# Seven-product pairs of an encoder layer: running sums kept in a PSUM bank instead of added on VectorE

## The chip, the cores and the metric

The kernel runs on one core of one Trainium2 chip. The time is device microseconds of that core, for one launch that computes the whole layer for both batches of requests. Engines are called as the profile calls them: PE is TensorE's matmul, PEld its loading of weights, DVE is VectorE, ACT is ScalarE, POOL is GpSimd, and SP is SyncE, whose queue issues nearly all transfers.

## The reference

One encoder layer is computed for two batches with the same weights: `x_prompt` with 512 tokens and `x_sample` with 1024 tokens, both 1024 channels wide. All of it is float32.

```python
def encoder_layer(x, norm_g, w_in, ..., w_o_a, w_o_b, w_out, t5_table):
    h = rmsnorm(x, norm_g)
    proj = h @ w_in
    qa, ka, va, za, qb, kb, vb, zb, ga, gb = jnp.split(proj, ...)
    ...
    oa = neighbourhood_attention(qa, ka, va, rpb_a) * jax.nn.silu(za)
    oa = oa @ w_o_a
    ...
    ob = window_gqa_attention(qb, kb, vb, t5_table, sink_b) * jax.nn.silu(zb)
    ob = ob @ w_o_b
    merged = jax.nn.sigmoid(ga) * oa + jax.nn.sigmoid(gb) * ob
    return x + merged @ w_out
```

What matters here are the dense products: `z` (8 chunks of 128 output channels), the gates `g` (16 chunks) and the output `w_out` (8 chunks), each with 1024 input channels.

## The kernel before, in words

**Precision.** Every float32 operand is split into a high part in the type that PE takes and the low rest (`split`, line 1161 onward: ACT makes the high part at L1167, DVE or POOL the rest at L1172). A block of 128 input channels then costs three matmuls: high weight by high data, high weight by low data, low weight by high data (`product`, L1284 to L1286). One such step of three is one operation of the planner.

**Stages.** Attention of the short batch, its dense phase, attention of the long batch, its dense phase. A dense phase computes the z chunks, then the gates, then the merge (`w_o_a`, `w_o_b`, times the gates), then the output. Two output chunks are taken together as a pair. With `CLASSIC_P = (4, 8, 4)` all pairs of the short batch are classic: one PSUM bank for each chunk and half of the tokens, eight steps each. With `CLASSIC_S = (1, 0, 2)` the long batch takes 3 z pairs, 6 gate pairs and 2 output pairs with seven products instead of eight (`pair_strassen`): a 2 by 2 block product in which weights and data are first summed, and the products are combined afterwards. These eleven are called Z1 to Z3, G0 to G5, O2 and O3.

**A pair of seven products.** The raw weights of two chunks (two tiles each) are loaded; four sums S are made of them, and the seven operands are split into five of the six `whi`/`wlo` buffers, so the next pair's first tile has one to itself. The data side is either the normalized input `hh`/`hl` itself or one of four sums T of its blocks (T0 to T3). For the z and gate pairs these were stored to DRAM in an earlier stage by `norm_pair` and are loaded by `stored_sums`, through the four buffers of tile U; for the output pairs `sums` makes them on DVE and POOL. A product has 512 columns and four steps, 12 matmuls. In the order of the weights the products are P0 to P6. Before the change each one has a PSUM bank of its own:

- P0 is copied by ACT into p1 (a U tile, L1354); result (0,0) is p1 + P1.
- u2 = p1 + P2, u3 = u2 + P3, u4 = u2 + P4, each a DVE add into a U tile.
- result (1,1) is u3 + P4, result (1,0) is u3 - P5, result (0,1) is u4 + P6.

In the output pairs (`seed`) the residual x is loaded into a C tile, the U value is added, then the bank. In the last pair P6 is cut into two halves of 256 columns, in two banks, so that the first half can be stored while the second is computed.

**What follows a result** (`post`). A z result goes through Silu on ACT, is multiplied with the attention output loaded into `ot` (two buffers; two loads, which are added first, for the chunks of Z2 and Z3) and is stored. A gate goes through Sigmoid and is stored. An output is stored.

**Order of the work.** `Flow` takes all operations with their dependences, priorities and estimated durations, and plans them ahead: whenever an engine is free in its plan, it takes the ready operation with the lowest priority number, and among equals the one created first. The resulting order of each engine is then fixed. A pair's operations all carry the pair's priority, its weights half a unit less, so a later pair's operation fills in where the earlier pair has nothing ready. Tiles with the tags in `IN_TURN` (weights, T, S, raw, U, C, ot) are given out strictly in the order in which they were created in the program. The plan keeps two engines off one PSUM value at the same time (`locked`): an engine waits until the other's operation on it has ended.

**Banks.** PSUM has eight banks, handed out by `ROTA = "ppxxxxxd"`: two called p, five called x, one d. `bank(next(tags))` takes the next name, so the name of a bank in a profile row tells products apart.

## Time and profile before

| what | us |
|---|---|
| median of three timed runs | 1146.3 |
| lowest and highest of them | 1145.42 and 1147.29 |
| span of the profiled execution, first to last instruction | 1144.7 |
| PE busy in it | 1133.8 |
| PEld, DVE, ACT, POOL busy | 985.8, 854.4, 644.9, 308.3 |
| pairs Z1 to G5 of the long batch | 800.2 to 971.6 |
| first product of O2 | 1103.23 |

The profile is of one execution; for it the page gives the span and no other time. A row of the timeline has the start in us, the length in us, the engine, the source line, the operation, output tile <- input tiles with shapes, and in brackets how long the engine stood idle before it and what ended that idle time. A row of the waits has the waiting engine and line, the one it waited for, the total in us, how often, and the longest. A row of the stretches has start:end and length, then for PE, PEld, DVE, ACT and POOL the busy time and the number of instructions, then PE's granted clock (1.00 is full), the busy share of the DMA engines, and GB/s. A row of a tile has the line, engine, operation and number of instructions, then shortest, median and longest in ns, then the first and last start. A row of the chain of waits has start, length and what it was. SPq is the queue of SP, where a transfer is issued; lines 1354 and 1161 are the lines of helpers and copies: L1161 is every two-operand add, subtract or multiply of the dense phases. Matmuls overlap: one with 512 columns is shown as 0.39 us long, but the next starts 0.23 us after it.

### The profile page before, as it was taken

How to read it: one execution, taken by the hardware profiler on the slowest of the kernel's cores; microseconds unless marked ns; L12 is line 12 of the kernel's file. 1: busy time of each engine (PE TensorE's matmuls, PEld its weight loads, DVE VectorE, ACT ScalarE, POOL GpSimd, SP SyncE). 2: the span in 40 equal slices, each digit the busy share in tenths (PEclk: the TensorE clock that was granted, in tenths of full speed). 3: DMA queues.
4: the chain of work that ended last, by engine and by line, in shares of the span. 5: the costliest groups of instructions: out<-in, count | busy, mean ns of one | idle time of the engine just before them, and what ended most of it. 6: DMA issues, size and time to landing. Idle time of an engine off the chain costs nothing.

```text
span 1144.7 us, 18482 instructions
## 1 busy us (share of the span) xinstructions
PE 1133.8 (99%) x6139; PEld 985.8 (86%) x6139; DVE 854.4 (75%) x1975; ACT 644.9 (56%) x1467; POOL 308.3 (27%) x413
## 2 busy tenths in 40 slices
PE   8999999999999999999999999999999999999998
PEld 6999988888888899999999888888888888788887
DVE  5888798497765468887778888865878755497984
ACT  5777987544433346665678988865534434343320
POOL 3653433000010054343333445330222210132110
PEclk9999999999999999999999999999999999999999
DMA  7854543488786422121221213226657335573072
GB/s 253 273 158 141 181 113 102 115 264 266 232 277 199 165 72 67 25 70 32 71 61 50 56 37 93 56 66 214 218 148 211 129 111 159 200 238 121 29 223 90
DMA packets 124705, 159.86 MB, mean 140 GB/s; under 512 B 28297, under 2 KB 66961, under 8 KB 124610
## 3 DMA queue, kind: packets, MB, share of 16 engines
q1 hardware_dynamic: 124610, 158.69, 45.4%
q8 instruction: 48, 0.79, 0.3%
q14 instruction: 47, 0.39, 0.1%
HBM read 121.93 MB, written 41.44 MB: 143 GB/s over the span
## 4 chain that ended last, share of the span: by engine, by line
PE 94%; DVE 2%; DMA 2%; ACT 1%; POOL 1%; issue 0%; SPq 0%; ACTq 0%; POOLq 0%
PE p L761 25%; PE x L1285 9%; PE x L1286 9%; PE x L1284 9%; PE x L1063 5%; PE x L1026 5%; PE x L934 4%; PE p L1284 4%; PE p L1285 4%; PE d L1284 4%; PE p L1286 4%; PE d L1286 4%; PE d L1285 4%; PE x L861 2%; DMA ot<-u_d 1%; DMA w<-in_w_att_dram 1%
## 5 line engine op out<-in xcount | busy, mean ns | idle before, releaser
L761 PE MATMUL p<-whi,hh 128*128 128x384 f32 x384 | 133.4, 348 | 0.0
L761 PE MATMUL p<-wlo,hh 128*128 128x384 f32 x384 | 133.1, 347 | 0.0
L761 PE MATMUL p<-whi,hl 128*128 128x384 f32 x384 | 132.4, 345 | 0.0
L978 ACT ACTIVATE sb<-sb,mx 128x384 f32<-128x384 f32 (+1 forms) x192 | 107.5, 563 | 22.4 <-DVE mx L969 22.2
L1167 ACT ACTIVATE whi<-raw 128x512 fp32r<-128x512 f32 (+1 forms) x140 | 81.1, 590 | 52.6 <-PE x L1285 26.2
L761 PE MATMUL p<-whi,hb 128*128 128x384 f32 x384 | 107.5, 347 | 0.0
L1172 POOL TENSOR_TENSOR wlo<-raw,whi 128x512 fp32r<-128x512 f32 (+1 forms) x29 | 40.9, 1413 | 242.4 <-ACT whi L1167 130.4
L1284 PE MATMUL x<-hh,whi 128*128 128x512 f32 x264 | 102.7, 389 | 0.0
L1285 PE MATMUL x<-hl,whi 128*128 128x512 f32 x264 | 102.7, 389 | 0.0
L1286 PE MATMUL x<-hh,wlo 128*128 128x512 f32 x264 | 102.7, 389 | 0.0
L1037 DVE TENSOR_TENSOR pp<-x,pp 128x512 fp32r<-128x512 f32 (+1 forms) x136 | 82.6, 638 | 18.9 <-ACT pp L1032 17.8
L1172 DVE TENSOR_TENSOR wlo<-raw,whi 128x512 fp32r<-128x512 f32 (+1 forms) x111 | 70.1, 645 | 30.5 <-ACT whi L1167 30.2
L1285 PE MATMUL x<-T,whi 128*128 128x512 f32 x224 | 87.5, 390 | 0.3 <-DVE T L1172 0.2
L1286 PE MATMUL x<-T,wlo 128*128 128x512 f32 x224 | 87.2, 389 | 0.0
L1284 PE MATMUL x<-T,whi 128*128 128x512 f32 x224 | 87.1, 389 | 0.0
L1032 ACT ACTIVATE pp<-x 128x512 fp32r<-128x512 f32 (+1 forms) x136 | 70.9, 560 | 22.8 <-PE x L1026 21.8
L799 POOL TENSOR_TENSOR rs_r<-rs_v,mhalf 128x4 f32<-128x4 f32 (+1 forms) x72 | 81.7, 1134 | 5.7
L1063 PE MATMUL x<-pp,v 128*128 128x256 f32 (+1 forms) x368 | 77.8, 324 | 0.8 <-DVE pp L1037 0.8
L792 POOL TENSOR_SCALAR rs_v<-ss 128x4 f32<-128x4 f32 (+1 forms) x72 | 26.2, 364 | 187.3 <-DVE ss L785 184.6
L761 PEld LDWEIGHTS p<-whi,hl 128*128 128x128 f32 x384 | 73.0, 190 | 1.3 <-issue 1.0
L761 PEld LDWEIGHTS p<-wlo,hh 128*128 128x128 f32 x384 | 73.0, 190 | 1.0 <-issue 0.5
L761 PEld LDWEIGHTS p<-whi,hh 128*128 128x128 f32 x384 | 73.0, 190 | 0.9 <-issue 0.5
(351 smaller groups left out, 2985.5 us busy)
## 6 DMA issues: line engine op xcount, KB each, us to landing
raw<-in_w_g_dram SPq DMA_DIRECT2D x76, 256.0 KB
w<-in_w_att_dram SPq DMA_DIRECT2D x46, 384.0 KB
ot<-o_d SPq DMA_DIRECT2D x36, 256.0 KB
g_d<-C SPq DMA_DIRECT2D x34, 256.0 KB
raw<-in_w_z_dram SPq DMA_DIRECT2D x32, 256.0 KB
raw<-in_w_out_dram SPq DMA_DIRECT2D x32, 256.0 KB
C<-g_d SPq DMA_DIRECT2D x24, 256.0 KB
out_dram<-C SPq DMA_DIRECT2D x23, 256.0 KB
```

The lines of the kernel that those rows point to most:

```text
L761: pe.matmul(ps.t[:, :GW], part[u](k), mv.t[:, c], start=k == 0 and m == 0, stop=k == KC - 1 and m == 2,)
L799: lambda e: nc.gpsimd.tensor_tensor(r.t[:, :nn], rv.t[:, :nn], mhalf[:, :nn], op=ALU.pow),
L978: act.activation(sb.t[:, :width], sb.t[:, :width], AF.Exp, bias=mx.t[:, i : i + 1], scale=-1.0, accum_out=sm.t[:, i : i + 1],)
L1026: pe.transpose(pt.t[:, u * P : (u + 1) * P], sbs[i].t[:, c * P : (c + 1) * P], ident)
L1032: lambda e, pt=pt, pp=pp, nn=nn: act.activation(pp.t[:, 0, :nn], pt.t[:, :nn], AF.Copy),
L1037: lambda e, pt=pt, pp=pp, nn=nn: dve.tensor_tensor(pp.t[:, 1, :nn], pt.t[:, :nn], pp.t[:, 0, :nn].bitcast(F32), op=ALU.subtract),
L1063: pe.matmul(out(), v.t[:, vs], mv(), start=first, stop=last)
L1167: (("act", ACT_(n)),), lambda e: act.activation(hi(), src(), AF.Copy), prio,
L1172: lambda e: engines[e].tensor_tensor(lo(), src(), hi().bitcast(F32), op=ALU.subtract), prio,
L1284: pe.matmul(out, hi.t[:, cs], mh(), start=first and k == 0, stop=False)
L1285: pe.matmul(out, hi.t[:, cs], ml(), start=False, stop=False)
L1286: pe.matmul(out, lo.t[:, cs], mh(), start=False, stop=last and k == len(ws) - 1)
```

## The change

In a pair of seven products P2, P3 and P5 are accumulated into the bank that holds P0. Between them ACT copies the bank to p1, u2 and u3, which are now plain copies. P4 moves ahead of P3 and has a second bank, from which result (1,1) reads; then P6 is accumulated into that bank, and result (0,1) is u2 plus it. Result (1,0) is read straight from the first bank. u4 and four DVE adds a pair are gone; the pair takes three banks instead of seven. In the last pair both halves of P6 go into the second bank. So that P5 can be added, T3 changes its sign, in `norm_pair` and in `sums`. A parameter `kept` comes with its branches, but no call sets it.

```diff
@@ norm_pair
-            (3, (1, 1), (1, 0), (1, 0)),
+            (3, (1, 0), (1, 1), (1, 0)),
@@ sums
-                step(3, lambda v=t[1]: v.t[:, :sn], (1, 0), 0, ALU.subtract, True, t[1])
-                step(3, lambda v=t[3]: v.t[:, :sn], (1, 0), 1, ALU.subtract, False)
+                after = done[k + 4, 0] if done else []
+                tt(
+                    lambda v=t[3]: v.t[:, :sn], h[1, 0, 0], lambda v=t[1]: v.t[:, :sn], ALU.subtract, sn, prio,
+                    new=[t[3]], use=[t[1]], after=after, hold=[hh],
+                )
+                step(3, lambda v=t[3]: v.t[:, :sn], (1, 0), 1, ALU.add, False)
@@ product
-        def product(ps, ws, movs, prio, first, last, after=(), n=nh):
+        def product(ps, ws, movs, prio, first, last, after=(), n=nh, at=0, again=False):
...
-                    out = ps.t[:, :n]
+                    out = ps.t[:, at : at + n]
...
+                    more = {"skip_group_check": True} if again else {}
@@ pair_strassen
-            p1, u2, u3, u4 = (tile_("U", 4, sn) for _ in range(4))
+            p1, u2, u3 = (tile_("U", 4, sn) for _ in range(3))
...
+            def mul(i, mov, ps=None, after=()):
+                fresh = ps is None
+                ps = ps or bank(next(tags))
+                h_reads.append(product(ps, w[i], mov, prio, fresh, True, [opened, *after], sn, again=not fresh))
                 return ps
...
+            def partial(out, ps):
...
+                return f.op(
+                    (("act", ACT_(sn, False)),), lambda e: act.activation(out.t[:, :sn], ps.t[:, :sn], AF.Copy), prio,
+                    new=[out], use=[ps],
+                )
...
-            result(0, 0, p1, mul(1, mov_h(1, 0)))
-            add(u2, p1, mul(2, mov_t(1)))
-            add(u3, u2, mul(3, mov_t(2)))
-            b = mul(4, mov_t(0))
-            add(u4, u2, b)
-            result(1, 1, u3, b)
-            result(1, 0, u3, mul(5, mov_t(3)), ALU.subtract)
+                x = mul(0, mov_h(0, 0))
+                o = partial(p1, x)
+                result(0, 0, p1, mul(1, mov_h(1, 0)))
+                x = mul(2, mov_t(1), x, [o])
+            o = partial(u2, x)
+            z = mul(4, mov_t(0))
+            x = mul(3, mov_t(2), x, [o])
+            o = partial(u3, x)
+            read = result(1, 1, u3, z)
+            x = mul(5, mov_t(3), x, [o])
...
+                post(1, 0, sn, x, True, prio)
             if not last:
-                result(0, 1, u4, mul(6, mov_h(1, 1)))
+                result(0, 1, u2, mul(6, mov_h(1, 1), z, [read]))
                 return
...
-                product(ps, w[6], movs, prio, True, True, n=nh // 2)
+                o = product(z, w[6], movs, prio, False, True, [read], nh // 2, s.start, True)
                 tt(
-                    lambda s=s: c.t[:, s], lambda s=s: c.t[:, s], lambda ps=ps: ps.t[:, : nh // 2], ALU.add, nh // 2,
-                    prio, psum=True, use=[ps], hold=[c], after=c.writers[:],
+                    lambda s=s: c.t[:, s], lambda s=s: c.t[:, s], lambda s=s: z.t[:, s], ALU.add, nh // 2,
+                    prio, psum=True, hold=[c, z], after=[*c.writers[:], o],
                 )
```

## The prediction

> **What bounds the kernel now.** I read the page first: span, busy shares, the chain of work that ended last. The span of this one execution is 1144.7 us; the three timed runs have a median of 1146.3, so I sum against the span and add 1.6 at the end.

> ```profile
> span 1144.7 us, 18482 instructions
> ...
> PE 1133.8 (99%) x6139; PEld 985.8 (86%) x6139; DVE 854.4 (75%) x1975; ACT 644.9 (56%) x1467; POOL 308.3 (27%) x413
> ...
> PE 94%; DVE 2%; DMA 2%; ACT 1%; POOL 1%; issue 0%; SPq 0%; ACTq 0%; POOLq 0%
> ```

> PE is busy 99% and carries 94% of the chain: TensorE is the bound, and 10.9 us of the span are not its work. Second, the waits of PE, over the whole span and from 785 us on (the dense stage of the 1024-token batch, the only one with pairs of seven products, since the short batch's setting is all classic).

> ```profile
> PE x L1629 <- DMA rb<-in_norm_row_dram: 4.4, 1, 4.4
> ...
> PE x L1285 <- DVE T L1172: 0.2, 1, 0.2
> ```

> The large wait is at the start of the program; in the stage that changes there is one, of 0.2 us. Third, the busy time by stretches, each one pair long, and the stretch where the gates give way to the merge.

> ```profile
> 819.30:838.30 19.00, 19.00 (x85) 15.74 (x84) 12.35 (x20) 5.71 (x12) 4.49 (x3) 1.00 0.64 191
> ...
> 970.00:990.00 20.00, 19.66 (x85) 15.44 (x84) 9.78 (x15) 6.86 (x12) 1.62 (x1) 1.00 0.80 282
> ```

> PE (third column) fills its pair wholly at granted clock 1.00. Only 970 to 990 is short: 85 matmuls where 20 us hold 20/0.227 = 88, and gaps that I add up in the timeline to 1.1 us. So DVE and ACT time in these pairs is free now, and no removed DVE add can shorten the end by itself. The most this change could win is that 1.1 us.

> **The change part by part.** I call the products of a pair P0 to P6 by their weight operand, and the pairs Z1 to Z3, G0 to G5, O2, O3: eleven.

> Removed: u2, u3 and u4 on DVE, and one add for the result c10.

> ```profile
> L1161 DVE TENSOR_TENSOR U<-U,x x21: 674/683/689, 815.4 to 1136.1; 128x512 f32<-128x512 f32 x21
> ...
> L1161 DVE TENSOR_TENSOR U<-U,p x7: 680/687/689, 817.2 to 966.7; 128x512 f32<-128x512 f32 x7
> L1161 DVE TENSOR_TENSOR U<-U,d x5: 672/683/689, 816.6 to 1118.3; 128x512 f32<-128x512 f32 x5
> ```

> 21+7+5 = 33 adds, three a pair; with c10's, 44 at 0.68 = 30 us of DVE. ACT gains two copies a pair, 22 at 0.60 = 13 us. Both lie beside PE's work (in Z2 DVE is busy 12.35 and ACT 5.71 of 19.00), so both count as nothing as busy time; what they cost or give through the order of the queues is counted below. Behind a copy in ACT's queue stand silus and the next weight splits, which wait for nothing new unless PE is late. The matmuls stay the same in number and form, so PE's work stays. The T3 sign swaps operands in a subtract of the same shape, and `sums` keeps two instructions for it: nothing either way. No DMA is added; x loads of c10 in O pairs stay.

> What it adds is **waits of PE on the evacuation**. Before, each product has its own bank. Now P2 waits for the copy of P0's sum, P3 for that of P2's, P5 for that of P3's, and P6 for the add of c11 that reads P4's bank. Behind a waiting matmul stands all of PE. The price of one such wait without cover:

> ```profile
> 1124.77 0.39 PE L1286 MATMUL x<-hh,wlo 128*128 128x512 f32 x1
> ...
> 1125.25 0.60 ACT L1354 ACTIVATE U<-x 128x512 f32<-128x512 f32 x1 [5.04 <-PE x L1286]
> ...
> 975.01 0.69 DVE L1172 TENSOR_TENSOR T<-ot,T 128x512 fp32r<-128x512 f32 x1 [0.67 <-ACT T L1167]
> ...
> 975.76 0.50 PE L1285 MATMUL x<-T,whi 128*128 128x512 f32 x1 [0.22 <-DVE T L1172]
> ```

> The last matmul of P0 starts at 1124.77; an idle ACT copies from 1125.25 to 1125.85; a result reaches a waiting PE 0.06 later (975.70 to 975.76). PE could go on at 1125.91 instead of 0.23 after the last start: **0.91 us**. Covers: P1 stands between P0 and P2, P4 between P2 and P3, each 2.72 us (two products from 800.23 to 805.67, quoted below), so the copy may be 1.8 late. Between P3 and P5 nothing of the pair is left; the planner takes whatever is ready, so two steps of the next pair's P0 (0.68 each, 1.36) if its weights are there. P6 has P5 (2.72) against one add of 0.69.

> *The end, O3.* No pair follows, so P3 to P5 is bare: 0.91.

> ```profile
> 1140.03 0.28 PE L1284 MATMUL p<-hh,whi 128*128 128x256 f32 x1
> ...
> 1140.28 0.42 DVE L1161 TENSOR_TENSOR C<-C,p 128x256 f32<-128x256 f32 x1 [0.80 <-PE p L1286]
> ...
> 1141.35 0.28 PE L1286 MATMUL p<-hh,wlo 128*128 128x256 f32 x1
> ...
> 1141.66 0.42 DVE L1161 TENSOR_TENSOR C<-C,p 128x256 f32<-128x256 f32 x1 [0.96 <-PE p L1286]
> ```

> Now the add of the first half (1140.28) runs while PE writes the second half into another bank. With both halves in one bank the planner's lock keeps DVE off until PE is done with the bank; the first add then moves behind 1141.63 and pushes the last by its 0.42. Bounds 0 and 0.42; I take 0.4, as the lock is in the code. End: **1.3**. [...]

> *The start, Z1.*

> ```profile
> 800.23 0.39 PE L1284 MATMUL x<-hh,whi 128*128 128x512 f32 x1
> ...
> 801.96 0.93 ACT L1167 ACTIVATE whi<-raw 128x512 fp32r<-128x512 f32 x2
> ...
> 805.67 0.39 PE L1284 MATMUL x<-T,whi 128*128 128x512 f32 x1
> ...
> 811.61 1.32 DVE L1172 TENSOR_TENSOR T<-U,T 128x512 fp32r<-128x512 f32 x2 [0.30 <-ACT T L1167]
> ...
> 812.34 0.60 ACT L1354 ACTIVATE U<-x 128x512 f32<-128x512 f32 x1
> ```

> P0 ended at 802.95, yet its copy came at 812.34: tile U has four buffers in turn, and the sixteen loads of the T sums stand first; the copy gets a buffer when DVE frees one (811.61+0.69 = 812.30). Today P2 goes on at 805.67 regardless. Then it must wait until 813.0, 7.3 us. Ready in between: P4 (2.72), and P0 and P1 of Z2, whose weights are made at 801.96 (5.44): 8.16. So no idle there, but this spends the later covers: 0.91 each before P3 and P5, less the 0.8 left over: **1.0**. Bounds 0, and 3 if P1 of Z2 isn't ready.

> *The lag, Z2 to G1.* Silu results wait for two loads each through two ot buffers.

> ```profile
> DVE ot L1161 <- DMA ot<-o_d: 11.7, 5, 3.9
> ...
> 840.80 0.39 PE L1286 MATMUL x<-hh,wlo 128*128 128x512 f32 x1
> ...
> 845.14 0.63 ACT L1387 ACTIVATE C<-C 128x512 f32<-128x512 f32 x1 [2.04 <-DVE C L1161]
> 845.68 0.58 ACT L1354 ACTIVATE U<-x 128x512 f32<-128x512 f32 x1
> ...
> 859.84 0.39 PE L1286 MATMUL p<-hh,wlo 128*128 128x512 f32 x1
> ...
> 865.69 0.58 ACT L1354 ACTIVATE U<-p 128x512 f32<-128x512 f32 x1
> ...
> 917.45 0.60 ACT L1354 ACTIVATE U<-x 128x512 f32<-128x512 f32 x1 [0.59 <-PE x L1286]
> ```

> DVE stands 11.7 us on the ot loads between 812 and 892; ACT stands on DVE; P0's copy stands behind that in ACT's queue. A copy 0.48 after the last matmul would be at 841.28 in Z3 and 860.32 in G0; it came 4.4 and 5.4 late. Free banks swallow that now; PE would stand for it less 0.4 to 1.8 of cover, at most 5.0 in all (a stall once taken makes the next smaller). Against it DVE loses 4 x 0.68 = 2.7 a pair. If both of Z2 and Z3 count, nothing is left; I count one, since DMA waits do not shrink with DVE work: 5.0-2.7 = **2.3**, bounds 0 and 5. In G3 the copy waits for PE itself (917.45): G2 to G5 cost 0.

> *The merge.* Its T tiles reuse those of the sums: T1 free after P2, T2 after P3, which now comes after P4.

> ```profile
> 963.40 0.63 ACT L1167 ACTIVATE T<-ot 128x512 fp32r<-128x512 f32 x1 [1.57 <-PE d L1285]
> ...
> 964.95 0.32 SPq L1537 DMA_DIRECT2D ot<-u_d  x1
> ...
> 967.11 4.66 DMA ot<-u_d
> ...
> 973.18 4.96 DMA ot<-u_d
> ```

> 963.40 becomes 2.72 later. Two ot buffers are taken in turn, so the load at 967.11 follows the one released there (964.95 becomes 967.7) by an SP issue: near 968.0. It feeds the next, at 973.18, and that the matmul after it: **0.9**. Bounds -1.1 (today's gaps gone) and 2.7.

> *O2.* The copy stands behind a split that waits for a late load.

> ```profile
> 1108.21 0.42 ACT L1167 ACTIVATE whi<-raw 128x256 fp32r<-128x256 f32 x1 [3.88 <-DMA raw<-in_w_out_dram]
> ...
> 1108.53 0.58 ACT L1354 ACTIVATE U<-x 128x512 f32<-128x512 f32 x1
> ...
> 1108.67 0.39 PE L1284 MATMUL x<-T,whi 128*128 128x512 f32 x1
> ```

> Done at 1109.11, plus 0.06, against 1108.67: **0.5**, bounds 0 and 0.5.

> Sum: 1.3+1.0+2.3+0.9+0.5 = 6.0. Span 1150.7, time 1152.3. All lower ends give about -0.2 (1146.1), all upper ends 12.5 (1158.8).

> **The rivals.** *Covered:* only the end shows, 1147.6 (+0.1%), not slower. Place: Z2 to G1. It decides where the relief of DVE brings the copies to within 1.8 us of PE. For it: 2.7 us a pair in a stretch where DVE has no slack, and a planner that fills gaps; against it: the waits on ot loads, and a planner whose order is fixed ahead and met loads later than planned. *Bare:* every bank re-entered shows its 0.91: 33 x 0.91 + 0.4 = 30.4, 1176.7. [...] Against bare: P1 and P4 lie between. *Faster:* needs more than 2.3 us, while the pairs hold 1.1. That DVE's adds do not go, or that the sums are not kept in one bank, nothing in the code suggests.

> **How the numbers follow.** About 0.2% (2.3 us) is what a measurement of this kernel tells from no change. Forecast, 1148.6 to 1159: 0.66; worse than 1159 short of bare 0.03; bare 0.03; covered, within 0.2%: 0.25; faster 0.03. Slower 0.72. The range 1147 to 1159 leaves out the two upper cases, the faster one and the lowest part of covered, some 2 in 10.

> **What would show it.** Right: PE waits on ACT U at P2, P3 or P5, about 0.9 in the last pair and above that in Z1 to G1; DVE some 30 us less busy; ACT 13 more; a first-half add behind the last matmul. P3 after P4 in the PE order. Wrong: no PE wait before 1120 us, or one at P6 on DVE that is larger than those on ACT, or fewer matmuls.

## The result, and the profile after

The changed kernel takes 1158.1 us (median of six runs, 1156.9 to 1159.5) against 1146.8 for the kernel before in the same session (six runs, 1145.4 to 1155.2): a ratio of 1.0095, with an interval of 1.0077 to 1.0113, so slower by 8.8 to 13.0 us. The forecast was 1152.3, in a range of 1147 to 1159. The direction was right and the time lies in the range; the size was too small, 6.0 us forecast and 10.4 to 11.3 found. The profiled execution has a span of 1155.1 us, 10.4 more than before.

The page of the changed kernel, its span, the busy time of the engines and their shares of the chain that ended last:

```profile
span 1155.1 us, 18395 instructions
...
PE 1137.8 (99%) x6139; PEld 985.6 (85%) x6139; DVE 830.1 (72%) x1933; ACT 654.4 (57%) x1489; POOL 299.7 (26%) x411
...
PE 80%; DVE 8%; DMA 6%; ACT 2%; issue 2%; POOL 1%; SPq 0%; DVEq 0%; ACTq 0%; POOLq 0%
```

PE has the same 6139 matmuls. DVE has 42 instructions and 24.3 us less, ACT 22 instructions and 9.5 us more. None of that made the kernel faster. What changed is the chain: PE's share of it fell from 94% to 80%, and DVE and DMA hold 14% of it. So there are now places where PE waits for work that hangs on DVE and on transfers. The waits of PE from 785 us on (waiting engine and line, what it waited for, total us, how often, longest) name them. In this kernel L1289 to L1291 are the matmuls, L1353 the copy of a bank into U, L1409 the gate functions, and L1161 the adds as before.

```profile
PE x L1289 <- ACT U L1353: 2.4, 2, 1.7
PE p L1289 <- ACT U L1353: 2.3, 1, 2.3
PE d L1289 <- ACT U L1353: 0.8, 1, 0.8
PE x L1289 <- ACT T L1167: 0.5, 1, 0.5
PE x L1290 <- DVE T L1172: 0.2, 1, 0.2
PE p L1290 <- DVE T L1172: 0.2, 1, 0.2
```

Before, this view had one row of 0.2. Now PE waits four times for the copy out of the bank that it wants to go on with (the three `ACT U` rows), and in no row for the add that reads P4's bank. Of 33 re-entries into P0's bank, 29 are hidden.

To see where the 10.4 us lie, I took from the timeline every start of a matmul that came later than its usual distance from the one before (0.227 us for 512 columns) and added up the excess by place:

| place | before | after | what the matmul waits for |
|---|---|---|---|
| Z1, 807.8 to 809.7 | 0 | 1.24 | T0's third block |
| Z2 and G0, 831 and 878 | 0 | 0.28 | |
| G0, P2 at 865.69 | 0 | 1.97 | copy of P0 |
| G1, P2 at 887.45 | 0 | 2.42 | copy of P0 |
| G1, 887.5 to 891.2 | 0 | 1.71 | nothing: half clock |
| merge | 1.00 | 1.39 | |
| O2, P2 at 1117.38 | 0 | 1.07 | copy of P0 |
| O3, P5 at 1145.56 | 0 | 0.96 | copy of u3 |
| last matmul start to end of span | 3.39 | 3.95 | |

The difference is 10.0 in the stage and 0.55 behind it, 10.6, against 10.4 of span. More than half of it, 6.1 us, lies in G0 and G1. The order of ACT there, from its timeline in the changed kernel (start, length, operation, and in brackets the idle time before it and what ended it):

```profile
880.92 0.64 ACT L1167 ACTIVATE whi<-raw 128x512 fp32r<-128x512 f32 x1 [1.21 <-PE d L1290]
884.42 0.42 ACT L1167 ACTIVATE whi<-raw 128x256 fp32r<-128x256 f32 x1 [2.86 <-DMA raw<-in_w_g_dram]
886.28 0.63 ACT L1409 ACTIVATE C<-C 128x512 f32<-128x512 f32 x1 [1.44 <-DVE C L1161]
886.82 0.58 ACT L1353 ACTIVATE U<-p 128x512 f32<-128x512 f32 x1
```

Three things stand in a row in this queue, and none of them has to do with the bank: a weight split that waits 2.86 us for its load, a gate function that waits 1.44 us for DVE's add, and only then the copy. P0's last matmul started at 882.08, so an idle ACT would have begun the copy at 882.56 (0.48 later, as in the prediction); it began at 886.82. The bank stood full and unread for 4.3 us, and ACT was idle for 3.3 of them. P1 fills PE until 885.03; what is left, with the copy itself, is the gap of 2.42. In G0 the same two waits are 2.25 (the load, 862.66) and 1.45 us (DVE's add, 864.52). PE's own rows in G1 (the last matmul of P0, the last of P1, the first of P2):

```profile
882.08 0.39 PE L1291 MATMUL p<-hh,wlo 128*128 128x512 f32 x1
...
884.80 0.39 PE L1291 MATMUL p<-hh,wlo 128*128 128x512 f32 x1
887.45 0.64 PE L1289 MATMUL p<-T,whi 128*128 128x512 f32 x1 [2.26 <-ACT U L1353]
887.89 0.63 PE L1290 MATMUL p<-T,whi 128*128 128x512 f32 x1
...
890.87 0.49 PE L1291 MATMUL p<-T,wlo 128*128 128x512 f32 x1
891.20 0.40 PE L1289 MATMUL p<-T,whi 128*128 128x512 f32 x1
```

After the wait the matmuls start 0.43 us apart instead of 0.23, up to 891.20. The stretches (the column behind the busy times is PE's granted clock) say why:

```profile
889.00:891.00 2.00, 2.00 (x6) 1.52 (x6) 0.54 (x1) 0.63 (x1) 0.00 (x0) 0.50 0.53 193
891.00:894.00 3.00, 3.00 (x15) 2.48 (x14) 0.76 (x2) 1.43 (x3) 0.00 (x0) 0.99 0.23 87
```

The clock was 0.50 for 3.4 us, from 887.65 to 891.06. This cost another 1.71 us, nearly as much as the wait in G0.

### The profile page after: what moved, and what is told of

Its sections match the earlier page's. It is cut to its first block, busy times and chain, and to the rows that moved or that the text cites. A ratio compares the mean times of both kernels' runs of the same rounds, so it can differ in the third digit from the quotient of the medians.

```text
span 1155.1 us, 18395 instructions
## 1 busy us (share of the span) xinstructions
PE 1137.8 (99%) x6139; PEld 985.6 (85%) x6139; DVE 830.1 (72%) x1933; ACT 654.4 (57%) x1489; POOL 299.7 (26%) x411
## 4 chain that ended last, share of the span: by engine, by line
PE 80%; DVE 8%; DMA 6%; ACT 2%; issue 2%; POOL 1%; SPq 0%; DVEq 0%; ACTq 0%; POOLq 0%
PE p L761 24%; PE x L1290 7%; PE x L1291 7%; PE x L1289 7%; PE x L1063 5%; PE x L1026 4%; PE x L934 4%; PE d L1289 4%; PE d L1291 3%; PE d L1290 3%; PE p L1290 3%; PE p L1289 3%; PE p L1291 3%; DVE S L1161 2%; PE x L861 2%
## 5 line engine op out<-in xcount | busy, mean ns | idle before, releaser
L1167 ACT ACTIVATE whi<-raw 128x512 fp32r<-128x512 f32 (+1 forms) x140 | 81.1, 592 | 65.0 <-PE x L1290 21.3
L1290 PE MATMUL x<-hl,whi 128*128 128x512 f32 (+1 forms) x264 | 102.1, 387 | 0.2 <-DVE hl L1172 0.2
L1289 PE MATMUL x<-hh,whi 128*128 128x512 f32 (+1 forms) x264 | 102.1, 387 | 0.0
L1291 PE MATMUL x<-hh,wlo 128*128 128x512 f32 (+1 forms) x264 | 102.0, 386 | 0.0
L1172 DVE TENSOR_TENSOR wlo<-raw,whi 128x512 fp32r<-128x512 f32 (+1 forms) x117 | 76.1, 662 | 25.8 <-ACT whi L1167 25.8
L1289 PE MATMUL x<-T,whi 128*128 128x512 f32 x232 | 90.7, 391 | 2.9 <-ACT U L1353 2.4
L1290 PE MATMUL x<-T,whi 128*128 128x512 f32 x232 | 90.5, 390 | 0.2 <-DVE T L1172 0.2
L1291 PE MATMUL x<-T,wlo 128*128 128x512 f32 x232 | 90.4, 390 | 0.0
L1172 POOL TENSOR_TENSOR wlo<-raw,whi 128x512 fp32r<-128x512 f32 (+1 forms) x23 | 31.2, 1366 | 171.2 <-DMA raw<-in_w_g_dram 114.6
```

What stands on the lines that cost most here:

```text
L1167: (("act", ACT_(n)),), lambda e: act.activation(hi(), src(), AF.Copy), prio,
L1172: lambda e: engines[e].tensor_tensor(lo(), src(), hi().bitcast(F32), op=ALU.subtract), prio,
L1289: pe.matmul(out, hi.t[:, cs], mh(), start=first and k == 0, stop=False, **more)
L1290: pe.matmul(out, hi.t[:, cs], ml(), start=False, stop=False, **more)
L1291: pe.matmul(out, lo.t[:, cs], mh(), start=False, stop=last and k == len(ws) - 1, **more)
```

## The experiments

**Theory:** the matmuls, the adds and the copies cost nothing as work. The cost is a set of single stalls, each where a copy out of the re-entered bank stands in ACT's queue behind something late (a weight load, a gate function that waits for DVE, which waits for `ot` loads). **Rival 1:** the new order of the products (P4 ahead of P3) disturbs the plan. **Rival 2:** each re-entry costs its own 0.9, and the places are chance. Each kernel is compared with the kernel before in the same session. The variants e1 to e5, e7 and e8 share one text with three lists of pairs: `ACC_X` (P0, P2, P3, P5 in one bank), `ACC_Z` (P6 in P4's bank) and `EARLY4` (P4 ahead of P3); a pair stands in them by its priority, 1 to 3 for Z1 to Z3, 4 to 9 for G0 to G5, 22 and 23 for O2 and O3. The diffs show what a setting comes to. In those kernels lines are shifted: the matmuls are L1296 to L1298, the copy L1358, the gate functions L1430, the adds L1166, the splits L1172 and L1177. "Gaps" is the sum of late matmul starts as in the table above.

**e1: the order and the sign alone.** Every product keeps its own bank, against the kernel before:

```diff
-            add(u3, u2, mul(3, mov_t(2)))
             b = mul(4, mov_t(0))
+            add(u3, u2, mul(3, mov_t(2)))
             add(u4, u2, b)
             result(1, 1, u3, b)
-            result(1, 0, u3, mul(5, mov_t(3)), ALU.subtract)
+            result(1, 0, u3, mul(5, mov_t(3)))
```

> Only the new order and sign: P4 goes ahead of P3 and T3 has its new sign, but every product has its own bank and DVE adds as before the change. Theory (PE waits on the ACT copies behind late work): no copy gates PE, so within 0.5 us of before, 1.000. Rival (the order itself costs, by the T tiles freed later for the merge): 0.9 to 2.7 us longer, all of it in the merge.

Measured: ratio 0.9998 (0.9989 to 1.0008), span 1143.7, gaps 0.79, nearly all in the merge. Rival 1 falls: order and sign cost nothing. So the order alone does no harm; for a gap like Z1's, P2 has to be held back as well, so that P4 is pulled forward.

**e2: P6 into P4's bank alone.** P0, P2, P3 and P5 keep their banks, the old order stays, u4 is gone:

```diff
-            add(u4, u2, b)
...
-            result(0, 1, u4, mul(6, mov_h(1, 1)))
+            result(0, 1, u2, mul(6, mov_h(1, 1), b, [read]))
```

> Only the second bank shared: P6 is accumulated onto P4's bank after result (1,1) has read it, u4 is gone; P2, P3 and P5 keep banks of their own and the order is the old one. Theory: what gates P6 is a DVE add; DVE was up to 8 us behind PE in Z2 to G1, so PE stands at P6 there, 1 to 4 us in all, and at the end 0.6 us from the half add that waits for the bank: 1.5 to 4.5 us, 1.001 to 1.004. Rival (only ACT copies cost): 0.6 us, 1.0005.

Measured: ratio 1.0039 (1.0024 to 1.0054), span 1148.5, gaps 4.19. Here PE does wait at P6 for the add that reads P4's bank; the waits of PE from 785 us on:

```profile
PE x L1296 <- ACT T L1172: 1.0, 1, 1.0
PE p L1296 <- DVE C L1166: 0.8, 1, 0.8
PE x L1296 <- DVE C L1166: 0.6, 2, 0.3
PE x L1297 <- DVE T L1177: 0.2, 1, 0.2
```

The wait of 0.8 is in Z1, where P4 ran late and only one step stood between it and P6 (P4's last matmul started at 816.20, P6's first at 818.09). DVE's queue there: the add (`C<-U,p`, the first of the two in its row) stands behind a u value, a sum of weights and u4.

```profile
815.36 0.68 DVE L1166 TENSOR_TENSOR U<-U,x 128x512 f32<-128x512 f32 x1
815.96 0.69 DVE L1166 TENSOR_TENSOR S<-raw,S 128x512 f32<-128x512 f32 x1
816.56 0.68 DVE L1166 TENSOR_TENSOR U<-U,d 128x512 f32<-128x512 f32 x1
817.35 1.28 DVE L1166 TENSOR_TENSOR C<-U,p 128x512 f32<-128x512 f32 x2
```

In the whole change there is no such wait. Of the 4.19 us, 1.09 are in Z1, 1.08 in Z2 and G0, and 2.02 in the merge, against 1.0 there before. The end is 0.55 longer than before, as in the whole change; in e3, where P6 has banks of its own, it is not.

**e3: P0, P2, P3, P5 in one bank, P6 in its own.** u4 stays on DVE:

```diff
-                result(0, 1, u2, mul(6, mov_h(1, 1), z, [read]))
+                result(0, 1, u4, mul(6, mov_h(1, 1)))
...
+            add(u4, u2, z)
```

> Only the first bank shared: P2, P3 and P5 accumulated onto P0 with ACT copies between, P4 ahead of P3; P6 has a bank of its own again and u4 is a DVE add. Theory: the stalls at G0, G1, O2 and the last pair stay, the half add at the end no longer waits: 8 to 11 us longer than before, 1.007 to 1.0095. Rival (the sum of both shared banks makes the loss, each alone is covered): under 4 us.

Measured: ratio 1.0090 (1.0068 to 1.0111), nearly the whole change's 1.0095; span 1151.1, gaps 8.84: 1.01 and 0.81 in G0, 2.59 at 882.06 in G1, 2.0 in the merge, 1.98 in O2. The ratio mixes two kinds of execution: two of the four (1156.6 and 1157.5 us) have a mean granted clock of 0.997, and two (1152.9, the profiled one, and 1153.7) have 1.000. Against the 1145.8 of the kernel before, the latter give 1.006 to 1.007. So the bank of the running sum carries most of the cost. What the second bank adds to it is the end of the program, 1.5 us. The gap at 882.06 is longer than the one of 2.42 in the changed kernel, but no half clock followed it; this is taken up below. In O3 there was no gap, and PE's timeline shows why (the last matmul of P3, the first of P6's first half, the first of P5):

```profile
1142.02 0.39 PE L1298 MATMUL x<-T,wlo 128*128 128x512 f32 x1
1142.24 0.28 PE L1296 MATMUL d<-hh,whi 128*128 128x256 f32 x1
...
1143.32 0.40 PE L1296 MATMUL x<-T,whi 128*128 128x512 f32 x1
```

P6 has a bank of its own, so nothing holds it, and nine of its matmuls fill the 1.08 us of the copy. In the whole change P6 waits for P4's bank to be read, hence for u3, hence for the same copy: the second shared bank takes the cover away from the first.

**e4: the same change, the copy of P0 first in ACT's queue.** It goes ahead of the gate function of the previous pair's result (0,1), and ahead of the second weight split of the next pair:

```diff
             x = mul(0, mov_h(0, 0))
             o = copy_out(p1, x)
+            for q in later:
+                q.after.append(o)
+            copied[:] = [o]
```

> The whole change, and in ACT's order the copy of P0 is put ahead of two things: the gate or silu of the pair before's result (0,1), and the split of the next pair's second weight tile. Theory: G0 (2.0 us), G1 (4.3 with the slow matmuls behind it) and O2 (1.1) are gone, left are Z1 1.2, the end 1.5, the merge 0.3: 3 us longer than before, 1.0027, at most 4.5. Rival (evacuation is short of capacity, and the stall moves to P3, P5 or P6): 7 us or more, with waits of PE at those products.

Measured: ratio 1.0053 (1.0038 to 1.0068), span 1150.4, gaps 6.38. ACT's timeline of e4 in G1:

```profile
882.46 0.60 ACT L1358 ACTIVATE U<-p 128x512 f32<-128x512 f32 x1 [0.90 <-PE p L1298]
882.95 0.62 ACT L1430 ACTIVATE C<-C 128x512 f32<-128x512 f32 x1
885.80 0.73 ACT L1172 ACTIVATE whi<-raw 128x256 fp32r<-128x256 f32 x2 [2.23 <-DMA raw<-in_w_g_dram]
```

The load is as late as ever (2.23 us), but the copy no longer stands behind it, and P2's gaps of 1.97 in G0, 2.42 in G1 and 1.07 in O2 are gone, with the half clock. This is the theory's main point, shown by a change of ACT's order alone. The total is not what was expected (3, at most 4.5): Z1 took 2.80 instead of 1.24 and the merge 1.97 instead of 1.39, and a wait of 0.65 came up in G0, ahead of P3, the kind that the rival names, but not its 7 us. Rival 2 falls here: 33 re-entries stay, and the stalls move with the queue.

**e5: the change in G2 to G5, O2 and O3 alone.** Z1 to G1 are as before.

```diff
-ACC_X = ACC_Z = EARLY4 = (1, 2, 3, 4, 5, 6, 7, 8, 9, 22, 23)
+ACC_X = ACC_Z = EARLY4 = (6, 7, 8, 9, 22, 23)
```

> The change in G2 to G5, O2 and O3 only; Z1 to G1 keep one bank for each product. Theory: the loss of the change lies in Z1 (1.2), G0 (2.0) and G1 (4.3); left are O2 1.1, the end 1.5 and the merge 0.3: 2.9 us longer than before, 1.0025, and no wait of PE between 800 and 960 us. Rival (each re-entry of a bank costs a little everywhere): six pairs of eleven, so about half of 10.4, 5 us or more.

Measured: ratio 1.0017 (1.0005 to 1.0029), span 1146.3, gaps 2.65: merge 1.42, O2 0.27, O3 0.97. None of the four gate pairs has a gap. What is late before 900 us makes the difference between this and the whole change.

**e7: the whole change with three `ot` buffers.** To pay for it in memory, U has three instead of four:

```diff
-        n_c, n_ot = (4, 2) if short else (5, 2)
+        n_c, n_ot = (4, 2) if short else (5, 3)
...
-            p1, u2, u3 = (tile_("U", 4, sn) for _ in range(3))
+            p1, u2, u3 = (tile_("U", 3, sn) for _ in range(3))
```

> The whole change with a third ot buffer and three U buffers instead of four (the change leaves three U values a pair). Theory (the lag of DVE and ACT in Z2 to G1 comes from attention outputs that are loaded late through two buffers): DVE's waits on ot fall from 11.9 us to under 6, the gaps at G0 and G1 shrink to under 2 us together, and the merge's gaps of 1.4 us go: 3 to 6 us longer than before, 1.003 to 1.005. Rival (the copies are late because of raw weight loads at ACT's head, 5.1 us, which a third ot buffer doesn't speed up): gaps at G0 and G1 as in the change, 9 us or more, 1.008.

Measured: ratio 1.0095 (1.0076 to 1.0113), as slow as the change; but the time went elsewhere. In the profiled execution (span 1151.9, the fastest of the four) DVE's waits between 812 and 892 us:

```profile
DVE ot L1166 <- DMA ot<-o_d: 2.7, 4, 1.1
```

They were 11.9 in the changed kernel and 11.7 before. G0's and G1's gaps are gone entirely; the merge keeps 0.95. This fits the theory that the `ot` loads are the root of the lag, but e7 alone does not show it: PE also came some 5 us later out of Z1, which gives DVE and ACT that much time to catch up. What came instead is in Z1, where T's loads and P0's copy share the U tiles, now three. ACT's timeline of e7:

```profile
812.40 0.63 ACT L1172 ACTIVATE T<-U 128x512 fp32r<-128x512 f32 x1 [1.05 <-DMA U<-t_d]
813.33 0.63 ACT L1172 ACTIVATE T<-U 128x512 fp32r<-128x512 f32 x1 [0.30 <-DMA U<-t_d]
814.73 0.63 ACT L1172 ACTIVATE T<-U 128x512 fp32r<-128x512 f32 x1 [0.77 <-DMA U<-t_d]
815.26 0.58 ACT L1358 ACTIVATE U<-x 128x512 f32<-128x512 f32 x1
```

The copy came at 815.26, 3.5 us later than in the changed kernel (811.8): PE had run out of products that it could pull forward, waited 2.45 us, and came back at half clock, which cost 1.7 (the mean clock from 815.8 to 821.5 is 0.70). Right behind that it stood once more, for 1.0 us, at the next re-entry (P3, for the copy of u2):

```profile
821.25 0.50 PE L1296 MATMUL x<-T,whi 128*128 128x512 f32 x1 [0.75 <-ACT U L1358]
```

The "2.71 at half clock" that the next expectation goes by is the sum of these two.

**e8: three `ot` and three U buffers, and Z1 as before the change.**

```diff
-ACC_X = ACC_Z = EARLY4 = (1, 2, 3, 4, 5, 6, 7, 8, 9, 22, 23)
+ACC_X = ACC_Z = EARLY4 = (2, 3, 4, 5, 6, 7, 8, 9, 22, 23)
```

> The changed kernel with three ot and three U buffers again, but pair Z1 in the form of before (a bank for each product, u4 on DVE, P4 behind P3); Z2 to O3 accumulate. In the run with three ot buffers 5.2 us stood in Z1 alone (a gap of 2.45 and 2.71 at half clock behind it) and none in Z2 to G1. Theory (each stall belongs to its place: a copy that is late because of what stands before it in ACT's queue): with no re-entered bank in Z1 the 5.2 us go, and what is left is the end (0.97 + 0.58), O2 (0.6) and the merge (0 to 0.9): span 1144.7 + 2.2 to 3.1 = 1147.3, time 1149, ratio 1.002. Rival (PE falls behind the planner's order somewhere in any case; a stall taken out shows up in the next pair, here Z2, whose T sums also come through three U buffers): again 5 us or more in Z2 to G1, span above 1151, ratio above 1.005.

Measured: ratio 1.0050 (1.0033 to 1.0067), span 1148.7, gaps 4.34. Z1's 5.2 us are gone and have not turned up in the next pairs: Z2 to G1 hold 0.49, with DVE's waits on `ot` at 6.3 us and ACT's on gate weights at 0.6 (5.1 in the changed kernel). Here PE had no late start out of Z1, so it is e8 that ties the lag to the buffers. It changes U and Z1 as well, and no run changes the `ot` buffers alone, so this much stays argued. This bears the theory out (each stall belongs to its place) against its rival, though the ratio is at the edge between the two, since O2 now took 2.06 in place of 0.6. ACT's timeline of e8 there:

```profile
1109.97 0.42 ACT L1172 ACTIVATE whi<-raw 128x256 fp32r<-128x256 f32 x1 [4.12 <-DMA raw<-in_w_out_dram]
1110.29 0.58 ACT L1358 ACTIVATE U<-x 128x512 f32<-128x512 f32 x1
```

This is the same shape once more: a split that waits for a load, and the copy behind it. By how much the load is late differs between the kernels (O2's gap was 0.27 to 2.06 in the changed kernel, e3, e5, e7 and e8); why, these runs do not settle. No version beat the kernel before by a measurable amount, and none can by much: it has 1.0 us of gaps in this stage.

**e6 and e9: what a gap does to the clock.** Into the kernel before, stalls of PE made by hand: k small ACT copies of a bank just written, then an in-place copy of the T tile that the next product reads. Nothing is left out; e6 has k from 0 to 13 in G2 to G5, e9 has k = 8 twelve times in G0 to G5.

```diff
                     if stall and k == len(ws) - 1:
+                        for _ in range(stall[0]):
+                            act.activation(pad, ps.t[:, :LEFT_PAD], AF.Copy)
+                        act.activation(stall[1](), stall[1]().bitcast(F32), AF.Copy)
```

> Before the change, with stalls of known length put in by hand in G2 to G5: after P2 and after P4 ACT copies 56 columns k times out of the product's bank and then copies the next product's first T block onto itself, and PE has to wait for it; k = 0, 3, 5, 6, 7, 8, 10, 13, unknown to the plan. Gaps between matmuls should rise from 0.9 to about 3.5 us. Theory (a gap of PE longer than about 2 us lowers the granted clock, as behind the 2.65 us gap in G1, and a 2.1 us gap does not): matmuls behind the gaps up to k = 5 run at 0.23 us each, those from some k between 6 and 8 on at 0.43 for 2 to 4 us. Rival (the slow matmuls of G1 come from busy transfers or memory, not from the gap): all gaps leave the matmuls behind them at 0.23 and the clock at 1.00.

> The kernel before with twelve equal stalls of PE made by hand, two in each of G0 to G5: eight small ACT copies of the bank just written, and one in-place ACT copy of the T tile that the next product needs. In the run with stalls of unequal length eight of these made a gap of 2.78 us. Adds only idle time to PE. Theory A (length alone decides whether PE comes back at half clock, and the two long gaps that were not followed by it were odd cases): nearly all of the twelve are followed by some 1.7 us of loss at half clock, span 1144.7 + 12 x 4.5 = about 1198. Theory B (where the gap falls against something that runs on its own decides as well): only some of them are followed by it, between 3 and 9 of 12, span 1183 to 1193, with gaps of equal length on both sides.

Measured: e6 had a span of 1170.2 and seven gaps of 1.48 to 4.03 (k = 0 left none); three of the seven were followed by half clock, those of 2.54, 2.78 and 4.03, while one of 3.28 was not. e9 had a span of 1200.2, eleven gaps of 2.78 and a first one of 7.93. Ten of the twelve were followed by half clock, at a cost of 1.6 to 2.1 us each, 17.2 in all; two gaps of 2.78 were not. By number and span this is nearer to A, but gaps of one length went both ways, which A does not allow. Three of them in e9, by the stretches behind them (the gaps end at 882.94, 901.08 and 929.01; the two columns at the end are the transfers):

```profile
884.00:887.00 3.00, 3.00 (x8) 2.32 (x8) 0.68 (x1) 0.36 (x1) 0.00 (x0) 0.50 0.49 183
901.70:904.00 2.30, 2.30 (x7) 1.82 (x6) 0.90 (x2) 0.15 (x1) 0.00 (x0) 0.50 0.00 0
929.50:932.50 3.00, 3.00 (x15) 2.45 (x14) 1.45 (x3) 0.29 (x1) 0.00 (x0) 1.00 0.00 0
```

```profile
882.94 0.50 PE L1285 MATMUL x<-T,whi 128*128 128x512 f32 x1 [2.62 <-ACT T L1291]
...
929.01 0.50 PE L1285 MATMUL x<-T,whi 128*128 128x512 f32 x1 [2.62 <-ACT T L1291]
```

The same 2.62 us of waiting, then a clock of 0.50 in one case and 1.00 in the other. The rival of e6 falls too: the second stretch has the half clock without any transfer. What tells the gaps apart is worked out in the last section.

## Why the prediction was right, and where it was too low

- **TensorE is the bound, and busy time of the others is free.** Right: the same 6139 matmuls, and 42 instructions less on DVE gave nothing. The change in busy time was smaller than forecast (24.3 against 30, 9.5 against 13). Part of it is in the rows: adds in a row start 0.60 apart though each is shown as 0.68 long (815.36, 815.96 and 816.56 in e2), and POOL has two instructions less (411 after 413) where DVE has lost 42 and not 44, so two seem to have moved over.
- **The end, 1.3.** Measured 1.51. The bare re-entry cost 0.96 against 0.91: the term lacked that the second matmul after a wait starts 0.34 later and not 0.23 (1145.56 and 1145.90 in O3). The first half's add moved behind the last matmul, as the planner's lock has it, and cost 0.55 (3.95 from the last matmul's start to the end, 3.39 before) against 0.4. No run here shows two engines in one bank, so what the end would be without the lock is not shown. The row of both adds in the changed kernel:

```profile
1151.48 0.75 DVE L1161 TENSOR_TENSOR C<-C,x 128x256 f32<-128x256 f32 x2 [2.18 <-PE x L1291]
```

- **Z1, 1.0.** Measured 1.24, for another reason, so that the size came near is luck. As forecast, P0's copy was late (811.8), PE filled the time with P4 and products of Z2, and the held-back P2 cost nothing. The two later re-entries, priced at 0.91 each, cost nothing either. What the step had left out: P4, pulled forward, needs T0, whose third block came late. P4's matmul on it, from PE's timeline of the changed kernel:

```profile
808.60 0.49 PE L1289 MATMUL x<-T,whi 128*128 128x512 f32 x1 [0.47 <-ACT T L1167]
```

- **The lag, Z2 to G1, 2.3.** This is the term that failed: 6.4 was measured (0.28 + 1.97 + 2.42 + 1.71), above its upper bound of 5. The mechanism was the one named in part: the copy stood behind a gate function that waited for DVE (1.45 and 1.44 us in G0 and G1). The other part, a weight split that waited for its load (2.25 and 2.86), the working had only for O2. e4 (copy moved ahead, gaps gone) shows that the queue makes the stalls; that `ot` loads are behind them rests on e8, together with e7. The places moved too: Z3, where the copy had been 4.4 late, has no gap, and G1, for which no lateness was read, has the largest. The size went wrong in two ways. First, 2.7 us were taken off for DVE's relief. The working itself said that waits on DMA do not shrink with DVE's work, and they did not: 11.7 before, 11.9 after (one execution each; with two `ot` buffers the variants range from 7.1 to 11.5, and e1, which keeps its adds, has 7.1). Without the deduction the step gives 5.0, and the gaps were 4.7; with the places moved, that they agree so well is partly luck. Second, the half clock behind the longer gap, 1.71, was in no term and no bound.
- **The merge, 0.9.** Measured 0.39 more than before, within its bounds; by which chain was not followed up. **O2, 0.5.** Measured 1.07: right place and chain (the split that waits 3.88 for its load, then the copy). Here a 0.5 that was given as an upper bound was too low, since it took the distance between the load and PE from the trace of before; e3 and e8 with 1.98 and 2.06 show how far that moves.
- **G2 to G5, nothing.** Right: no gap from 891.2 to 989 us in the changed kernel, and none in these pairs in e5.
- **The rivals.** *Covered* had the relief of DVE as its condition, which did not come. *Bare* wanted a stall at each of 33 re-entries; four showed one. *Faster* is out by the interval. Of the signs named in advance, the PE waits on `ACT U` at P2 and P5, the last pair's 0.9 and the first half's add were there; in Z1 PE waited for T0 instead.

Together the terms gave 6.0 where 10.6 came by the table; 4.1 of the 4.6 that are missing belong to the lag.

## What to carry to other kernels

A bank that is accumulated further after being copied out turns the copy into part of TensorE's path, so what counts is not the copy's 0.6 us but what stands ahead of it in its engine's queue: look there for instructions that wait for loads or for another engine, and put the copy first, or leave such products their own banks, as here, where banks were free and the adds that were saved cost nothing. Freed time on an engine was no cover here for a delay that comes from transfers; count only the part of its lag that is its own work (24.3 us of DVE were freed, and its waits on `ot` were 11.9 after 11.7). And in these runs a gap on TensorE of 2.4 us or more was often, not always (in ten of e9's twelve), followed by a half clock that cost another 1.6 us or more.

## What the runs showed of the hardware

**Half clock after short gaps.** In e9 the ten stretches at half clock began at different distances from the gap, some before PE was back and some up to 1.0 us after. The granted clock itself, read in stretches of 0.02 us, steps on a grid. It falls at 870.06, 883.71, 900.78, 911.02, 938.32, 955.39, 965.63, 992.94, 1010.00 and 1020.24, and rises 3.41 us later each time (6.83 after the first fall). All these times lie within 0.01 us of multiples of 3.413 us from one another; the first fall and the last are 150.18 apart, 44 times 3.413. So do the steps in e6, in the changed kernel (it falls at 887.65 and, behind the last matmul, at 1153.88, 78 times 3.413 later) and in e7, each run with an origin of its own. With the periods so laid, the idle time in the emptiest period of each gap, for both runs:

| run | followed by half clock | not followed |
|---|---|---|
| e9, eleven gaps of 2.78 and one of 7.93 | 2.39, 2.48, 2.49, 2.65, 2.67, 2.72, 2.78, 2.78, 2.78, 3.41 | 1.85, 1.94 |
| e6, gaps of 1.48 to 4.03 | 2.23, 2.78, 3.24 | 1.18, 1.31, 1.85, 2.01 |

The gap of 2.59 in e3, which no half clock followed, fits. The only fall of the clock in that run's trace is at the end of the program:

```profile
1150.40:1150.42 0.02, 0.00 (x0) 0.00 (x0) 0.00 (x0) 0.00 (x0) 0.00 (x0) 1.00 0.00 0
1150.42:1150.44 0.02, 0.00 (x0) 0.00 (x0) 0.00 (x0) 0.00 (x0) 0.00 (x0) 0.62 0.00 0
```

If the steps of e3 lie 3.413 us apart as in the other runs, this lays the grid there: 78 periods of 3.413 us before it, at 884.2, a period ends within the gap (882.3 to 884.9) and divides it into 1.9 and 0.7. In the two executions of e3 with a mean clock of 0.997 a gap may have met the grid otherwise; they have no trace, so that is not shown. The grid does not explain every spread: of e7's four executions the shortest, 1153.7 us, has a mean clock of 0.998 and the longest, 1158.3, has 0.999, and one of the changed kernel's six has 1.000 and still took 1158.0. What spreads those stays open.
